# A convolution's first activation chunk moved from SyncE's DMA queue to ScalarE's

## The chip, the cores and the metric

The kernel runs on one core of a Trainium2 chip. TensorE multiplies matrices into PSUM; VectorE, ScalarE and GpSimd do elementwise work; SyncE only issues DMAs here. ScalarE and GpSimd can issue DMAs too, each into a queue of its own, and all queues use the same 16 DMA engines of the core. The metric is the device time of one execution in microseconds.

## The reference

A 3x3 convolution with zero padding, without bias, and then the maximum over 2x2 windows: the input `x` is 16 images of 64 channels of 64x64 in float32, the weights are 128x64x3x3, the output is 16x128x32x32.

```
conv[b, co] += weight[co, ci, kh, kw] * x_pad[b, ci, kh:kh+h, kw:kw+w]
output[b, c, i, j] = max(conv[b, c, 2*i:2*i+2, 2*j:2*j+2])
```

## The kernel before

Two images lie side by side on the 128 partitions (64 channels each), so TensorE works on two row halves at a time (the two "lanes" 0 and 1 in the order). Each of the eight pairs of images is cut into four chunks of 16 image rows, 32 chunks in all, numbered 0 to 31. The weights are not used as they come: sums and differences of their three kernel rows are formed first (the blocks G0, G1, G2, D0, D2, GM, GP), turned by TensorE (`T`), and copied back from PSUM as `wt` (`TV`). A chunk is done in one of two ways, given by the string `SEQ`. A W chunk uses sums and differences of image rows (E, S and V, tiles `we`, `ws`, `wv`), and takes four products, P0 to P3. A K chunk takes its rows as they are, cast to bfloat16 (`kx`), and takes five products (PAa, PAb, PBa, PBb, PR). The products of even output rows collect in one PSUM bank (A), those of odd rows in another (B). ScalarE copies bank A (`EV`, and `SE` as a seed into bank B), VectorE takes the maximum of the two (`MX`), ScalarE copies the odd columns (`OD`) and VectorE takes the maximum with the even ones (`CM`). `ST` stores.

The order of all work is written out by hand in the string `ORDER` (lines 16 to 80). Each token adds its instructions, so the order of the tokens is the order in which each engine and each queue meets its work; between engines semaphores do the rest. What the change and the prediction touch stands at its head:

- `LW` loads the weights (`wraw`, line 533) through SyncE.
- `c.X:e` forms block X on engine e (v VectorE, a ScalarE), line 196 or 191. GS is a sum (`gsum`) of which GM and GP are made.
- `LX.n` loads chunk n. For a W chunk it goes into the tile `wx`, line 262, on SyncE. Chunk 1 is the first W chunk: 17 rows, 544 KB. For K chunks 0 and 2 it goes into `kf`, line 268; chunk 0, the first five-product chunk, is loaded in two halves, `LX.0a` (288 KB) and `LX.0b` (256 KB). There the ending `:a` already chose ScalarE's queue, but no token used it.
- `E.1:v` is VectorE's first operation on chunk 1 (`we<-wx`), `V.1:v` the next one (`wv<-wx`). `P2.1.0` and `P2.1.1`, the first products, need E.1.
- `SE.1.0` seeds a bank. Where the bank has held nothing of the kind before, TensorE first writes zeros to it (`L430`) from the tile `zeros`.
- `XO.0b:a` and `XO.0a:v` cast chunk 0 to bfloat16 on ScalarE and VectorE.
- `CP.3` has ScalarE copy rows of W chunk 3 into a PSUM bank (line 287), for VectorE to read.

VectorE's order at the start is: the sum GS, D0, GM, D2, E.1, GP, V.1, the copy of GP (line 242), the cast XO.0a, two more copies. SyncE's is: weights, W chunk 1, chunk 0 in two halves, W chunk 3, chunk 2, and so on. The function `paced` makes loads wait for work far behind them; the loads named here have nothing to wait for.

Before the loop TensorE runs eight matmuls of ones (line 500). The table that ScalarE needs for its operations is loaded by an instruction that stands ahead of its first operation.

Of the kernel before, what the change touches and what calls it, by code (L numbers as in the profile page):

```python
# [13 lines left out]
SEQ = "KWKWWKWWWKWWWWKWWWKWWWWKWWWKWWWW"  # L14
ADDED = ()
ORDER = """
LW c.g1:a c.GS:v c.D0:v LX.1 c.GM:v c.D2:v LX.0a c.g0:a T.G0:0 T.GM:1 T.G1:2 E.1:v c.g2:a T.D2:3
TV.GM:a TV.G0:a T.G2:4 TV.D2:a LX.0b LX.3 P2.1.0:5 P2.1.1:6 TV.G2:a c.GP:v SE.1.0:7 V.1:v T.D0:1
LX.2 SE.1.1:0 T.GP:3 LX.4 TV.GP:v XO.0b:a XO.0a:v P0.1.1 P0.1.0 PAa.0.0a:4 PAa.0.1a:3 S.1:g P3.1.0
P3.1.1 TV.D0:v LX.8 XE.0a:a CP.3:1 PAa.0.1b PAb.0.0a TV.G1:v E.3:v S.3:v EV.1.1 EV.1.0 XE.0b:a  # L20
PAa.0.0b PAb.0.1a MX.1.1 PBa.0.1a:2 PBa.0.0a:6 PAb.0.0b PAb.0.1b V.3:g PBb.0.0a PBb.0.1a LX.6 XE.2:a
# [62 lines left out]
def kernel(  # L84
# [7 lines left out]
    nc = tc.nc  # L92
    FP32 = mybir.dt.float32
    BF16 = mybir.dt.bfloat16
# [13 lines left out]
    const = ctx.enter_context(tc.tile_pool(name="const", bufs=1))  # L108
# [16 lines left out]
    def behind(inst, other):  # L125
        if other is not None:
            tc.add_manual_dep(inst.ins, other.ins.name, SYNC, reason="order")
# [7 lines left out]
    def rows_of(p, lo, hi):  # L135
        return x[2 * p : 2 * p + 2].rearrange("b c h w -> (b c) h w")[:, lo:hi, :]

    def chunk(s):

        p, q = place[s]  # L140
        same = any(place[t] == (p, q - 1) and SEQ[t] == SEQ[s] for t in range(N))
        lo = 2 * R * q + 1 if same else max(0, 2 * R * q - 1)
        return p, lo, min(H, 2 * R * (q + 1) + 1)

    def half(s):
        return 2 * R * place[s][1] + R + 1
# [18 lines left out]
    wq = const.tile([CO, 7, 2, 2, CI], BF16)  # L165
    wt = const.tile([128, 7 * K, CO], BF16)
    gsum = const.tile([CO, 3, CI], FP32)
    zeros = const.tile([128, 512], BF16)
    nc.vector.memset(zeros, 0.0)
    ident = const.tile([128, 128], BF16)  # L170
    make_identity(nc, ident)
    wv = wraw.rearrange("a (c k) -> a k c", k=K * K)

    def ring(t, k):
# [69 lines left out]
            nc.vector.tensor_copy(out=dst, in_=src)  # L244


    kf = {}
    done = {}
    AHEAD = {"W": 12, "K": 13}

    def paced(s, inst):

        for l in (0, 1):
            behind(inst, done.get((s - AHEAD[SEQ[s]], l)))
        if SEQ[s] == "K" and s < AHEAD["K"] and s not in kf:
            behind(inst, done["head"])

    def load(s, part, e):
        p, lo, hi = chunk(s)
        if SEQ[s] == "W":  # L260
            t = wx[p % NWX]
            paced(s, nc.sync.dma_start(out=t[:, lo + 1 : hi + 1, :], in_=rows_of(p, lo, hi)))
            return
        if s not in kf:
            kf[s] = const.tile([128, hi - lo, W], FP32, name=f"kf_{s}")
        a, b = {"": (lo, hi), "a": (lo, half(s)), "b": (half(s), hi)}[part]
        q = nc.scalar if e == "a" else nc.sync
        paced(s, q.dma_start(out=kf[s][:, a - lo : b - lo, :], in_=rows_of(p, a, b)))

    def load_cast(s):  # L270
# [242 lines left out]
    for token in ORDER.split():  # L513
        what, _, at = token.partition(":")
        name, *args = what.split(".")
        if name in PRODUCTS:
            s, l = int(args[0]), int(args[1][0])
# [20 lines left out]
        elif name == "LX":  # L538
            load(int(args[0].rstrip("ab")), args[0].lstrip("0123456789"), at)
        elif name == "LK":  # L540
            load_cast(int(args[0]))
        elif name == "CP":
            lift(int(args[0]), int(at))
        elif name in ("XO", "XE"):
            to_bf16(int(args[0].rstrip("ab")), args[0].lstrip("0123456789"), int(name == "XO"), at)
        elif name in ("KS", "S", "E", "V"):
            f = rs_cast if name == "S" and int(args[0]) in ADDED else None
            (f or {"KS": ks, "S": rs, "E": re, "V": rv}[name])(int(args[0]), at)
        elif name in ("Ve", "Vo"):
            rv_half(int(args[0]), at, int(name == "Vo"))  # L550
        elif name == "SA":
            rs_add(int(args[0]))
        elif name == "ST":
            l, part = (int(args[1][0]), args[1][1:]) if len(args) > 1 else (None, "")
            store(int(args[0]), l, part, at)
        else:
            s = int(args[0])
            l, part = (int(args[1][0]), args[1][1:]) if len(args) > 1 else (None, "")
            if name in ("SE", "SEv"):
                bank["B", s, l] = int(at)  # L560
                seed(s, l, name[2:])
                continue
            if name in ("OD", "CM", "RM"):
                {"OD": odd, "CM": colmax, "RM": pairmax}[name](s, l, part)
            else:
                {"EV": evac, "MX": rowmax}[name](s, l)
# [36 lines left out]
```

## Time and profile before

| | us |
|---|---|
| Median of 3 runs | 104.27 (104.04 to 104.47) |
| The profiled execution | 103.89 |
| Its span, first to last instruction | 102.1 |
| TensorE busy | 95.6 |
| VectorE busy | 90.0 |
| ScalarE busy | 89.6 |
| GpSimd busy | 80.8 |

The profile's times count from the span's start. A timeline row gives the start, the length, the engine, the line, the operation with the tiles written and read (`out<-in`), and in square brackets the idle time of the engine before it with what ended it. `SPq` and `ACTq` are the queues of SyncE and ScalarE; the length of a DMA row is the time that its issue took. A row of a DMA list gives the size and the median time from the start of the issue to the landing. A row of a stretch gives its ends, its length, the busy time of PE, PEld (weight loads), DVE (VectorE), ACT (ScalarE) and POOL (GpSimd) with their instructions, TensorE's granted clock, the busy share of the DMA engines, and GB/s.

### The profile page before, as it was taken

The numbers are of one execution on the slowest core, as the hardware profiler recorded it, in microseconds if no ns is written. First come the engines' busy times: TensorE is split into PE (matmuls) and PEld (weight loads), VectorE is DVE, ScalarE is ACT, GpSimd is POOL, SyncE is SP. The second block draws the span as 40 slices with busy tenths as digits, with TensorE's granted clock in tenths as the row PEclk, the third lists the DMA queues.
The fourth block names the chain that finished last, engine by engine and source line by source line (L and its number), as shares of the span: only waits on it lengthen the run. The fifth ranks groups of instructions, "written<-read, shape, count | busy, mean of one in ns | idle before, by whom it ended". The sixth has DMA issues, their size and how long they took to land.

```text
span 102.1 us, 2481 instructions
## 1 busy us (share of the span) xinstructions
PE 95.6 (94%) x870; PEld 52.3 (51%) x870; DVE 90.0 (88%) x176; ACT 89.6 (88%) x200; POOL 80.8 (79%) x63
## 2 busy tenths in 40 slices
PE   6698999999999999999999999999999999999940
PEld 2155954555555567565555575555444446455310
DVE  1596999999989999999999999778989999998780
ACT  5597999888999999998899999999998988999930
POOL 5005998999599969999998999999971999999000
PEclk9999999999999999999999999999999999999999
DMA  2989999849940699999999971898769955302353
GB/s 42 343 235 414 418 419 335 181 113 356 263 122 0 165 219 324 250 322 328 255 404 350 377 287 28 251 251 219 282 213 311 340 179 180 128 32 74 132 182 103
DMA packets 13789, 24.07 MB, mean 236 GB/s; under 512 B 1104, under 2 KB 9680, under 8 KB 13776
## 3 DMA queue, kind: packets, MB, share of 16 engines
q1 hardware_dynamic: 12624, 22.16, 64.8%
q0 software_dynamic: 864, 1.56, 8.8%
q10 hardware_dynamic: 288, 0.20, 0.6%
q8 instruction: 7, 0.11, 0.4%
q14 instruction: 6, 0.05, 0.1%
HBM read 17.07 MB, written 8.39 MB: 249 GB/s over the span
## 4 chain that ended last, share of the span: by engine, by line
PE 84%; DVE 6%; DMA 3%; ACT 3%; issue 1%; ACTq 0%; DVEq 0%
PE acc L405 84%; DMA wraw<-in_weight_dram 3%; DVE wq L196 2%; ACT ev L420 1%; DVE wv L196 1%; ACT od L463 1%; DVE o L472 1%; DVE acc L440 1%; DVE we L196 1%; DVE gsum L196 0%; ACT acc L287 0%; ACT acc L436 0%; DVE wt L242 0%; DVE o L482 0%; ACTq L436 0%
## 5 line engine op out<-in xcount | busy, mean ns | idle before, releaser
L405 PEld LDWEIGHTS <-wt 64*128 64x128 bf16 x840 | 50.0, 94 | 40.6 <-issue 3.0
L405 PE MATMUL acc<-wv,wt 64*128 64x504 bf16 (+1 forms) x288 | 63.4, 377 | 0.5 <-DVE wt L242 0.5
L196 POOL TENSOR_TENSOR wv<-wx 128x1024 bf16<-128x1024 f32 x21 | 49.3, 2363 | 1.0 <-PE acc L405 0.4
L440 DVE TENSOR_TENSOR acc<-acc,ev 128x512 f32<-128x512 f32 x64 | 43.6, 692 | 2.7 <-ACT ev L420 1.4
L405 PE MATMUL acc<-kx,wt 64*128 64x504 bf16 (+6 forms) x216 | 38.6, 350 | 0.0
L405 PE MATMUL acc<-we,wt 64*128 64x512 bf16 (+1 forms) x144 | 36.9, 376 | 0.1
L405 PE MATMUL acc<-ws,wt 64*128 64x512 bf16 (+1 forms) x144 | 35.0, 377 | 0.2 <-DVE acc L440 0.2
L420 ACT ACTIVATE ev<-acc 128x512 f32<-128x512 f32 x48 | 28.8, 605 | 1.5 <-PE acc L405 1.2
L436 ACT COPY acc<-acc 128x512 f32<-128x512 f32 x48 | 28.2, 591 | 1.3 <-DVE o L472 0.4
L472 DVE TENSOR_TENSOR o<-acc,od 128x256 f32<-128x256 f32 x64 | 25.3, 414 | 2.1 <-ACT od L463 1.7
L463 ACT COPY od<-acc 128x256 f32<-128x256 f32 x64 | 23.0, 377 | 2.5 <-PE acc L405 1.2
L196 POOL TENSOR_TENSOR ws<-wx 128x512 bf16<-128x512 f32 x12 | 15.2, 1274 | 9.8 <-DVE kx L193 6.8
L196 POOL TENSOR_TENSOR we<-wx 128x512 bf16<-128x512 f32 x10 | 12.8, 1276 | 2.0 <-DVE ks L196 1.2
L405 PE MATMUL acc<-ks,wt 64*128 64x504 bf16 (+1 forms) x48 | 12.9, 376 | 0.0
L422 ACT COPY ev<-acc 128x512 f32<-128x512 f32 x16 | 9.3, 595 | 1.0 <-PE acc L405 0.8
L291 DVE TENSOR_TENSOR we<-acc,wx 128x512 bf16<-128x512 f32 x11 | 7.5, 683 | 1.2 <-ACT acc L287 1.1
L291 DVE TENSOR_TENSOR ws<-acc,wx 128x512 bf16<-128x512 f32 x11 | 7.5, 679 | 0.0
L287 ACT COPY acc<-wx 128x512 f32<-128x512 f32 x11 | 6.7, 606 | 0.6 <-DMA wx<-in_x_dram 0.6
L500 PE MATMUL acc<-const-bfloat16-1.0 128*128 128x512 bf16 x8 | 3.3, 585 | 0.8 <-PEq L584 0.8
L196 DVE TENSOR_TENSOR ks<-kx 128x512 bf16<-128x512 bf16 x8 | 4.0, 512 | 0.0
L196 DVE TENSOR_TENSOR wv<-wx 128x1024 bf16<-128x1024 f32 x3 | 3.7, 1217 | 0.0
L272 POOL DMA_DIRECT2D kx<-in_x_dram x6 | 3.5, 586 | 0.0
(28 smaller groups left out, 21.7 us busy)
## 6 DMA issues: line engine op xcount, KB each, us to landing
out_dram<-o SPq DMA_DIRECT2D x30, 256.0 KB, 3.5
wx<-in_x_dram SPq DMA_DIRECT2D x12, 512.0 KB, 7.1
wx<-in_x_dram SPq DMA_DIRECT2D x6, 544.0 KB, 5.1
wx<-in_x_dram SPq DMA_DIRECT2D x6, 480.0 KB, 7.7
kx<-in_x_dram POOLq DMA_DIRECT2D x3, 256.0 KB, 7.5
kf<-in_x_dram SPq DMA_DIRECT2D x1, 512.0 KB, 7.8
kx<-in_x_dram POOLq DMA_DIRECT2D x2, 240.0 KB, 7.8
wraw<-in_weight_dram SPq DMA_DIRECT2D x1, 288.0 KB, 3.0
```

Source lines behind the costliest of these rows:

```text
L196: inst = eng[e].tensor_tensor(out=out, in0=in0, in1=in1, op=op)
L272: paced(s, nc.gpsimd.dma_start(out=kx_of(p)[:, lo:hi, :], in_=rows_of(p, lo, hi)))
L287: nc.scalar.copy(out=acc[bank], in_=wrow(s, 0))
L291: nc.vector.tensor_tensor(out=t, in0=lifted[s], in1=wrow(s, 1), op=op)
L405: yield lambda kw=kw, o0=o0, o1=o1, c0=c0, c1=c1: nc.tensor.matmul(acc[t][:, i0:i1, o0:o1], wt[l * CI : l * CI + CI, K * BLOCKS[block] + T ...
L420: inst = nc.scalar.mul(t, acc[bank["A", s, l]], -1.0)
L422: inst = nc.scalar.copy(out=t, in_=acc[bank["A", s, l]])
L436: nc.scalar.copy(out=acc[b], in_=acc[bank["A", s, l]])
L440: nc.vector.tensor_tensor(out=t, in0=t, in1=ev[s, l], op=MAX)
L463: nc.scalar.copy(out=od[s, l][:, i0:i1], in_=acc[bank["B", s, l]][:, i0:i1, 1::2])
L472: done[s, l] = nc.vector.tensor_tensor(out=outs(s)[:, l, i0:i1], in0=acc[bank["B", s, l]][:, i0:i1, 0::2], in1=od[s, l][:, i0:i1], op=MAX,)
L500: nc.tensor.matmul(acc[n], ones[:, 0:128], ones, start=True, stop=True, skip_group_check=True)
```

## The change

The token `LX.1` becomes `LX.1:a`, and the two halves of chunk 0 move ahead of it. `load` learns to choose the queue for W chunks too. The tile `zeros` is no longer set by VectorE's memset but by a ScalarE multiplication by zero, which is now ScalarE's first operation, so the table load stands ahead of it and the DMA issue of chunk 1 behind both. SyncE's order becomes: weights, chunk 0 in two halves, W chunk 3, chunk 2, and so on as before. The order of the compute instructions on TensorE and GpSimd is unchanged; VectorE has one fewer and ScalarE one more.

```diff
 ORDER = """
-LW c.g1:a c.GS:v c.D0:v LX.1 c.GM:v c.D2:v LX.0a c.g0:a T.G0:0 T.GM:1 T.G1:2 E.1:v c.g2:a T.D2:3
-TV.GM:a TV.G0:a T.G2:4 TV.D2:a LX.0b LX.3 P2.1.0:5 P2.1.1:6 TV.G2:a c.GP:v SE.1.0:7 V.1:v T.D0:1
+LW LX.0a LX.0b LX.1:a c.g1:a c.GS:v c.D0:v c.GM:v c.D2:v c.g0:a T.G0:0 T.GM:1 T.G1:2 E.1:v c.g2:a
+T.D2:3 TV.GM:a TV.G0:a T.G2:4 TV.D2:a LX.3 P2.1.0:5 P2.1.1:6 TV.G2:a c.GP:v SE.1.0:7 V.1:v T.D0:1
...
-    zeros = const.tile([128, 512], BF16)
-    nc.vector.memset(zeros, 0.0)
     ident = const.tile([128, 128], BF16)
     make_identity(nc, ident)
+    zeros = const.tile([128, 512], BF16)
+    nc.scalar.mul(zeros, nc.const_aps.tensor(1.0, [128, 512], BF16), 0.0)
...
+    queue = {"s": nc.sync, "a": nc.scalar}
...
         if SEQ[s] == "W":
             t = wx[p % NWX]
-            paced(s, nc.sync.dma_start(out=t[:, lo + 1 : hi + 1, :], in_=rows_of(p, lo, hi)))
+            q = queue[e or "s"]
+            paced(s, q.dma_start(out=t[:, lo + 1 : hi + 1, :], in_=rows_of(p, lo, hi)))
             return
...
-        q = nc.scalar if e == "a" else nc.sync
+        q = queue[e or "s"]
         paced(s, q.dma_start(out=kf[s][:, a - lo : b - lo, :], in_=rows_of(p, a, b)))
```

## The prediction

> **What bounds the kernel now.** I read the page's head, then the chain of waits in order of time, then TensorE's own waits, then the first ten microseconds by engine, by DMA landing and by stretch.
>
> ```profile
> span 102.1 us, 2481 instructions
> PE 95.6 (94%) x870; PEld 52.3 (51%) x870; DVE 90.0 (88%) x176; ACT 89.6 (88%) x200; POOL 80.8 (79%) x63
> ```
>
> ```profile
> 0.74 3.02 DMA wraw<-in_weight_dram
> ...
> 3.79 0.51 DVE gsum L196
> 4.29 1.58 DVE wq L196 x3
> 5.87 0.60 DVE we L196
> 6.47 0.53 DVE wq L196
> 7.00 1.07 DVE wv L196
> ...
> 8.13 0.37 DVE wt L242
> 8.50 36.38 PE acc L405 x350
> ```
>
> ```profile
> 8.50:96.10 87.60, 87.55 (x826) 49.14 (x827) 81.97 (x160) 82.12 (x186) 79.49 (x49) 1.00 0.77 243
> ```
>
> The chain of waits says that the first 8.5 us are one unbroken string: the weights' load, then VectorE alone, step after step without a gap, until TensorE starts on its long run. The stretch 8.50 to 96.10 (its first number is the length, the second PE's busy time) shows TensorE busy 87.55 of 87.60 us at full clock (1.00). So the kernel is a start of 8.5 us, a TensorE run with nothing to take out, and a tail. Whatever moves 8.50 moves the end by as much; what speeds up VectorE, ScalarE or a DMA behind 8.50 is worth nothing unless it is in one of TensorE's few small gaps.
>
> TensorE's own waits in the list for 8.4 to 96 us are one row, and it is the start itself:
>
> ```profile
> PE acc L405 <- DVE wt L242: 0.5, 1, 0.5
> ```
>
> The change works on what VectorE reads in those 8.5 us. Its timeline and the landings (the last number: microseconds from issue to landing), with the issues of SyncE (SPq) and ScalarE's work:
>
> ```profile
> 3.79 0.51 DVE L196 TENSOR_TENSOR gsum<-wraw 128x192 f32<-128x192 f32 x1 [2.65 <-DMA wraw<-in_weight_dram]
> ...
> 5.26 0.61 DVE L196 TENSOR_TENSOR wq<-wraw 128x256 bf16<-128x256 f32 x1
> 5.79 0.68 DVE L196 TENSOR_TENSOR we<-wx 128x512 bf16<-128x512 f32 x1
> ```
>
> ```profile
> 0.74 0.37 SPq L533 DMA_DIRECT2D wraw<-in_weight_dram  x1
> 1.17 0.42 SPq L262 DMA_DIRECT2D wx<-in_x_dram  x1
> 1.64 0.90 SPq L268 DMA_DIRECT2D kf<-in_x_dram  x2
> ```
>
> ```profile
> wraw<-in_weight_dram SPq DMA_DIRECT2D x1, 288.0 KB, 3.0
> ```
>
> ```profile
> wx<-in_x_dram SPq DMA_DIRECT2D x1, 544.0 KB, 4.4
> kf<-in_x_dram SPq DMA_DIRECT2D x1, 288.0 KB, 5.8
> ```
>
> ```profile
> kf<-in_x_dram SPq DMA_DIRECT2D x1, 256.0 KB, 6.2
> ```
>
> The weights land at 0.74 + 3.0 = 3.76 (the chain's end of that step), VectorE starts 0.03 later. The first W chunk (the tile `wx`, 544 KB) lands at 1.17 + 4.4 = 5.57, and its first reader, the operation E.1 (`we<-wx`), starts at 5.79, straight after the operation before it: the chunk is 5.79 - 0.03 - 5.57 = 0.19 us early. That is all the slack there is. The two halves of the first five-product chunk (`kf`) land at 1.64 + 5.8 = 7.44 and about 1.64 + 0.45 + 6.2 = 8.3.
>
> **The change, part by part.**
>
> *The zeros.* VectorE loses a memset; ScalarE gains a multiply of 128x512, behind the table load.
>
> ```profile
> 0.87 0.27 DVE L169 MEMSET zeros<- 128x256 uint32 x1 [0.87 <-PEq L584]
> ```
>
> ```profile
> 0.74 1.28 ACT L191 ACT_TABLE_LOAD   x1 [0.74 <-PEq L584]
> 3.79 1.75 ACT L191 CAST wq<-wraw 128x256 bf16<-128x256 f32 x3 [1.76 <-DMA wraw<-in_weight_dram]
> ...
> 9.68 0.59 ACT L287 COPY acc<-wx 128x512 f32<-128x512 f32 x1 [0.56 <-DMA wx<-in_x_dram]
> ```
>
> ```profile
> 7.46 0.38 PE L430 MATMUL acc<-zeros 128*128 128x512 bf16 x1
> ```
>
> The memset's 0.27 us lie in VectorE's wait for the weights (2.65 us after it), so its removal gains 0. ScalarE is free from 2.02 to 3.79; a multiply of about 0.6 us (its 128x512 copy at 9.68 took 0.59) and one DMA issue (0.42 by SyncE's row) end by about 3.1. If that cover were gone the casts of the weights would start late; 0.7 us of it are left. The only reader, TensorE's zero matmul, comes at 7.46. Cost 0. Moving the identity's making on GpSimd one line up changes no order there. Cost 0.
>
> *SyncE's queue.* With the W chunk gone the `kf` halves are issued at 1.17 and 1.64 instead of 1.64 and 2.11, and every later load 0.47 earlier. Who gains? The halves' readers stand behind E.1, V.1 and the step at 8.13 on VectorE and behind the seeds on ScalarE; TensorE's row above shows it waiting for none of them. The next W chunk is waited for, by the copy at 9.68 (0.56 us); an earlier landing there gives ScalarE up to 0.56 us back, but TensorE runs without a wait across it. Gain 0, with at most a few tenths in later gaps.
>
> *The W chunk on ScalarE's queue.* This is the one part on the path. It is issued behind the table load, so at 2.02 or a little later instead of 1.17. I take 2.05: the last DMAs of the kernel show that ScalarE's queue issues while the instruction just ahead of it still runs.
>
> ```profile
> 98.94 0.27 ACT L463 COPY od<-acc 128x128 f32<-128x128 f32 x1 [0.82 <-DVE o L482]
> 98.94 0.96 ACTq L495 DMA_DIRECT2D out_dram<-o  x2
> ```
>
> If it must wait for the multiply's end it is 2.6, 0.55 later. The first data follow an issue by about 1 us (weights issued at 0.74; the stretch 1.50 to 1.75 below is the first with any), so the chunk's data begin at about 3.05. In the rows below the last number is GB/s, the one before it the DMA engines' busy share.
>
> ```profile
> 1.50:1.75 0.25, 0.25 (x2) 0.15 (x1) 0.00 (x0) 0.25 (x1) 0.17 (x2) 1.00 0.03 9
> 1.75:2.00 0.25, 0.25 (x2) 0.00 (x0) 0.00 (x0) 0.25 (x1) 0.21 (x1) 1.00 1.96 240
> 2.00:2.25 0.25, 0.25 (x2) 0.15 (x1) 0.00 (x0) 0.02 (x1) 0.00 (x0) 1.00 0.65 55
> 2.25:2.50 0.25, 0.25 (x2) 0.06 (x1) 0.00 (x0) 0.00 (x0) 0.00 (x0) 1.00 0.19 65
> ...
> 4.50:5.00 0.50, 0.00 (x0) 0.00 (x0) 0.50 (x2) 0.50 (x2) 0.00 (x0) 1.00 1.21 239
> 5.00:5.50 0.50, 0.44 (x5) 0.27 (x6) 0.50 (x2) 0.50 (x1) 0.00 (x0) 1.00 0.84 184
> 5.50:6.00 0.50, 0.48 (x8) 0.31 (x8) 0.50 (x2) 0.26 (x2) 0.00 (x0) 1.00 0.67 123
> 6.00:6.50 0.50, 0.44 (x6) 0.35 (x7) 0.50 (x2) 0.50 (x2) 0.00 (x0) 1.00 0.97 177
> ...
> 9.00:9.50 0.50, 0.50 (x12) 0.40 (x10) 0.22 (x1) 0.13 (x1) 0.50 (x1) 1.00 1.04 426
> ```
>
> In the queue of before the chunk's data went alone, straight behind the weights. Now `kf` stands there, and the chunk comes from a second queue onto the same 16 DMA engines. How two queues share is seen where GpSimd's queue (q0) and SyncE's (q1) both have work, in the microsecond 17 to 18 (packets, MB, share of the engines):
>
> ```profile
> q0 software_dynamic: 59, 0.12, 63.5%
> q1 hardware_dynamic: 46, 0.17, 44.0%
> ```
>
> They take turns, about packet by packet (59 to 46), and the shares add to the whole: nothing is moved on the side. A packet is one partition's line of a load (46 packets of 0.17 MB are 3.7 KB each), 128 in the chunk and 128 in each `kf` half, so by the time the chunk is through, the first half has gone as well: 288 + 544 + 288 = 1120 KB, against 832 KB before. That gives the two ends of its landing.
> Upper end: before, exactly those 1120 KB had landed with the first `kf` half at 7.44, slow stretch of 4.5 to 6.5 included (123 to 239 GB/s). E.1 would wait 7.44 - 5.76 = 1.68 us.
> Lower end: no slow stretch. Up to 2.5 some 0.25 x (9 + 240 + 55 + 65) = 92 kB had moved; the other 1055 kB at the full rate of 426 GB/s take 2.5 us: 5.0, and with an allowance of 0.3 to 0.5 from last byte to landing, 5.3 to 5.5. E.1 would wait for nothing.
> The slow stretch of before is the very time in which `kf` was moved (between the landings at 5.57 and 8.3), and `kf` is moved again, only sooner; but part of the slowness may belong to the time and not to the data. I take the middle, 6.45, and a wait of 6.45 - 5.76 = 0.7 us.
>
> [...]
>
> *What follows a late E.1.* Behind it on VectorE stand the GP block's sum, V.1 and the copy at 8.13, all on the chain, so 8.50 becomes 9.20. TensorE's first products need E.1's result directly. ScalarE's seeds wait for those. VectorE and ScalarE take their later idle time (the 0.56 above) as cover, TensorE has none. The removed slack is 0.19, the new wait 0.7, all on the path.
>
> Sum: 0 (zeros) + 0 (SyncE) + 0.7 (W chunk) = +0.7 us. The profiled execution took 103.89 (span 102.1 and 1.79 around it), so 104.6 by it; it lay 0.38 under the median of the runs, and on the median of 104.27 the sum is 104.95.
>
> **The rivals.**
>
> *In time after all.* The chunk lands by 5.76: the lower end above. For it: the slow stretch may not come back, and 5.3 to 5.5 leaves 0.2 to 0.4. Against it: any slow half microsecond uses that up. Time: 104.27.
>
> *The table load holds nothing back (the change does not do what it says).* If ScalarE's queue runs past the table load, the issue comes at about 0.8 and the chunk takes turns with the weights themselves. The weights are then through when most of the 832 KB are: 544 KB more before them, 1.3 us at 426 GB/s, at most 5.57 - 3.76 = 1.8. All of the chain moves by that: 105.6 to 106.1, say 105.85. For it: the 98.94 rows, where the DMA did not wait for the copy ahead. Against it: two instructions stand ahead here, and the table load starts at 0.74 together with SyncE's DMA issue, as something that the queue itself does. [...]
>
> *The table load costs more than its row.* ScalarE might be held beyond 2.02, with the issue at 3 or later, and its casts delayed too: landing past 7.2 and 105.8 or more. The row of 3.79 only shows it free by then. [...]
>
> *Faster.* The weights stall: 55 and 65 GB/s from 2.00 to 2.50, against 426 when the queue flows. If that is because a 544 KB load is being put in the queue right behind them (issued 1.17 to 1.59), a 288 KB one there could give back up to that half microsecond: weights at 3.26, chain 0.5 earlier, 103.75. It decides only if the W chunk is in by 5.26, so it needs the share of the engines to be better than turn by turn, or no slow stretch. Against it: those are the first data of all, and a cold start would be as slow with any successor.
>
> **How the numbers follow.** Forecast (late W chunk, 0.3 to 1.7 us): 0.50, own range 104.5 to 105.9. In time: 0.22. Past the table load: 0.12. Longer table load: 0.04. Faster: 0.12. Half a per cent, 0.52 us, is about what a measurement tells here. Slower by more: three quarters of the forecast and both table-load cases, 0.38 + 0.16 = 0.54. Within: 0.22 and the rest of the forecast, 0.34. Faster: 0.12. Predicted 104.95. The range leaves out most of "faster" and the far ends: 103.9 to 106.0.
>
> **What would show it.** Right: an ACTq issue of `wx` at 2.0 to 2.1; its landing over 4 us later, at 6 or more; in VectorE's timeline, E.1 with a wait for the DMA of `wx` in front; TensorE's run beginning about 9.2 instead of 8.50 and as long as before; the chain's string broken by that DMA. Wrong: E.1 straight behind the operation before it (in time); the ACTq issue at 0.8 and the weights landing near 5 (past the table load); weights before 3.5 (faster). The sum would also fail if TensorE's run itself became longer or shorter than 87.6 us.

## The result, and the profile after

| | before | changed |
|---|---|---|
| Median of 20 runs each | 104.16 us | 105.64 us |
| Lowest and highest | 103.52 to 105.29 | 104.47 to 107.34 |
| The profiled execution, and its span | 103.89, 102.1 | 105.81, 103.9 |

The changed kernel is slower: the ratio is 1.0121, with a 95% interval from 1.0093 to 1.015, so about 1.3 us. The ratio is that of the means without each kernel's slowest executions (those over 1.5% above its fastest), and so not quite the quotient of the two medians. The twenty runs of the changed kernel fall into groups: three lie at 104.47 to 104.83, the rest at 105.39 and above, with nothing in between. The profiled execution is one of the second group.

The queues of the changed kernel come first. ScalarE's timeline:

```profile
0.73 1.28 ACT L171 ACT_TABLE_LOAD   x1 [0.73 <-PEq L586]
0.80 0.38 ACTq L264 DMA_DIRECT2D wx<-in_x_dram  x1
2.03 0.63 ACT L171 ACTIVATE zeros<-const-bfloat16-1.0 128x512 bf16<-128x512 bf16 x1
4.98 1.75 ACT L191 CAST wq<-wraw 128x256 bf16<-128x256 f32 x3 [2.33 <-DMA wraw<-in_weight_dram]
```

The load of the W chunk stands behind the table load and the multiplication in ScalarE's order, and is issued at 0.80, while the table load runs and 1.2 us before the multiplication begins. So it is issued beside SyncE's load of the weights (0.74), not behind it. The two loads' landings (last number, from the start of the issue):

```profile
wx<-in_x_dram ACTq DMA_DIRECT2D x1, 544.0 KB, 4.9
wraw<-in_weight_dram SPq DMA_DIRECT2D x1, 288.0 KB, 4.2
```

The weights take 4.2 us where they took 3.0. The W chunk is in at 0.80 + 4.9 = 5.7, hardly later than before (5.57). What the DMA engines did between 3 and 4 us (packets, MB, share of the engines; q10 is ScalarE's queue, q1 SyncE's):

```profile
q10 hardware_dynamic: 58, 0.25, 62.2%
q1 hardware_dynamic: 54, 0.12, 35.3%
```

They took turns, 58 packets to 54, and since a packet of the chunk is nearly twice as long (0.25 MB in 58 packets are 4.3 KB each, 0.12 MB in 54 are 2.2), the weights had a third of the engines, 35.3% against 62.2%. Now VectorE and TensorE:

```profile
4.99 0.50 DVE L196 TENSOR_TENSOR gsum<-wraw 128x192 f32<-128x192 f32 x1 [4.99 <-DMA wraw<-in_weight_dram]
...
6.97 0.70 DVE L196 TENSOR_TENSOR we<-wx 128x512 bf16<-128x512 f32 x1
...
10.16 0.36 DVE L242 TENSOR_SCALAR wt<-acc 128x384 bf16<-128x384 bf16 x1 [0.83 <-PE acc L229]
```

```profile
0.78 3.57 PE L502 MATMUL acc<-const-bfloat16-1.0 128*128 128x512 bf16 x8 [0.78 <-PEq L586]
6.23 1.83 PE L229 MATMUL acc<-ident,wq 128*128 128x128 bf16 x15 [1.88 <-ACT wq L191]
7.99 1.39 PE L407 MATMUL acc<-we,wt 64*128 64x512 bf16 x6
...
10.53 0.82 PE L407 MATMUL acc<-wv,wt 64*128 64x512 bf16 x6 [0.49 <-DVE wt L242]
```

The same groups of TensorE in the kernel before:

```profile
5.04 1.40 PE L229 MATMUL acc<-ident,wq 128*128 128x128 bf16 x15 [0.97 <-ACT wq L191]
6.53 0.82 PE L405 MATMUL acc<-we,wt 64*128 64x512 bf16 x6
```

VectorE starts 4.99 - 3.79 = 1.20 us later, and E.1 stands straight behind the operation before it: it waits for no W chunk. A second loss follows. TensorE's first 15 transposes take 1.83 us instead of 1.40 and its first six products 1.39 instead of 0.82, as at a lower clock. The trace's record of TensorE's clock bears this out: its first stretch of full clock begins at 9.19 us in the changed kernel and at 3.65 in the kernel before. At 10.16 VectorE has waited 0.83 us for TensorE. TensorE's long run begins at 10.53 instead of 8.50: 2.03 us later, of which 1.20 are the weights and 0.83 this. In the chain of waits, what follows the weights is now ScalarE's casts and TensorE's slow transposes and products, where before it was VectorE's work. From 10.80 to 19.20 it runs through GpSimd, whose first operation there starts 2.02 us later than before (10.80 against 8.78). It ends with the same steps as before, at 98.67 for the last three products against 96.89, so 1.78 of the 2.03 arrive:

```profile
0.74 4.22 DMA wraw<-in_weight_dram
...
4.98 1.20 ACT wq L191 x2
...
6.23 1.83 PE acc L229 x15
8.06 1.32 PE acc L407 x4
...
10.80 1.27 POOL ws L196
...
19.25 27.43 PE acc L407 x250
...
98.67 0.83 PE acc L407 x3
```

```profile
96.89 0.83 PE acc L405 x3
```

(The first of these two fences is the changed kernel, the second the kernel before.)

### The profile page after: what moved, and what is told of

Read it like the earlier page. It is cut to its first block, busy times and chain, and to the rows that moved or that the text cites. A ratio compares the mean times of both kernels' runs of the same rounds, so it can differ in the third digit from the quotient of the medians.

```text
span 103.9 us, 2481 instructions
## 1 busy us (share of the span) xinstructions
PE 96.5 (93%) x870; PEld 52.7 (51%) x870; DVE 90.0 (87%) x175; ACT 90.4 (87%) x201; POOL 80.8 (78%) x63
## 4 chain that ended last, share of the span: by engine, by line
PE 78%; POOL 7%; DMA 4%; ACT 4%; DVE 2%; issue 2%; DVEq 0%; ACTq 0%
PE acc L407 75%; DMA wraw<-in_weight_dram 4%; POOL wv L196 4%; POOL ws L196 2%; PE acc L229 2%; ACT wq L191 1%; ACT ev L422 1%; POOL kx L274 1%; ACT od L465 1%; DVE o L474 1%; DVE acc L442 1%; ACT acc L289 0%; ACT acc L438 0%; DVE o L484 0%; DVE kx L193 0%
## 5 line engine op out<-in xcount | busy, mean ns | idle before, releaser
L407 PE MATMUL acc<-we,wt 64*128 64x512 bf16 (+1 forms) x144 | 37.4, 386 | 0.0
L196 DVE TENSOR_TENSOR gsum<-wraw 128x192 f32<-128x192 f32 x1 | 0.5, 501 | 5.0 <-DMA wraw<-in_weight_dram 5.0
L229 PE MATMUL acc<-ident,wq 128*128 128x128 bf16 x21 | 2.5, 285 | 1.9 <-ACT wq L191 1.9
```

The costliest lines, as they stand in the source:

```text
L196: inst = eng[e].tensor_tensor(out=out, in0=in0, in1=in1, op=op)
L229: nc.tensor.transpose(tp[:, (j - lo) * 128 : (j - lo + 1) * 128], wq[:, BLOCKS[m]].rearrange("a i j c -> a (i j c)")[:, (j - lo) * CI : (j ...
L407: yield lambda kw=kw, o0=o0, o1=o1, c0=c0, c1=c1: nc.tensor.matmul(acc[t][:, i0:i1, o0:o1], wt[l * CI : l * CI + CI, K * BLOCKS[block] + T ...
```

## The experiments

**The price of sharing, by a smaller share.** Only 9 of the chunk's 17 rows go by ScalarE's queue, the other 8 by SyncE's right behind the weights.

```diff
-LW LX.0a LX.0b LX.1:a c.g1:a ...
+LW LX.1b LX.0a LX.0b LX.1a:a c.g1:a ...
...
+            a, b = {"": (lo, hi), "a": (lo, half(s)), "b": (half(s), hi)}[part]
-            paced(s, q.dma_start(out=t[:, lo + 1 : hi + 1, :], in_=rows_of(p, lo, hi)))
+            paced(s, q.dma_start(out=t[:, a + 1 : b + 1, :], in_=rows_of(p, a, b)))
```

> Only the first 9 of the W chunk's 17 rows (288 KB) go by ScalarE's queue at 0.80, the other 8 by SyncE's right behind the weights. Theory (turn by turn, 8 packets of each load on a DMA engine): between the weights' packets stand the same number of packets, each of 93 ns instead of 168, so the weights are late by about 8 x 93 ns = 0.7 us instead of 1.2 to 1.3: landing at 4.4 to 4.5, and the time about 0.7 us above before, more if TensorE starts cold. Rival (the delay does not hang on the bytes, but on a second queue being there): landing at 4.9 to 5.0 as in the changed kernel.

The weights' landing in its chain of waits:

```profile
0.74 3.49 DMA wraw<-in_weight_dram
```

They land at 4.23: 0.47 us late instead of 1.20, with half the bytes beside them. The expectation was 0.7; the direction and the order of size are those of packets taking turns, and a delay that comes with the mere presence of a second queue (4.9 to 5.0) is excluded. The ratio of times is 1.0071 (1.0022 to 1.0121), but it is not the price of sharing alone: in this profile, too, the transposes take 1.82 us and the first products 1.46, and VectorE waits 0.99 us for TensorE.

**The load truly held.** The W chunk's issue waits for the end of the multiplication.

```diff
-    nc.scalar.mul(zeros, nc.const_aps.tensor(1.0, [128, 512], BF16), 0.0)
+    zeroed = nc.scalar.mul(zeros, nc.const_aps.tensor(1.0, [128, 512], BF16), 0.0)
...
-            paced(s, q.dma_start(out=t[:, lo + 1 : hi + 1, :], in_=rows_of(p, lo, hi)))
+            inst = q.dma_start(out=t[:, lo + 1 : hi + 1, :], in_=rows_of(p, lo, hi))
+            if e == "a":
+                behind(inst, zeroed)
+            paced(s, inst)
```

> The W chunk's issue on ScalarE's queue waits for the end of the multiplication by zero, so it comes at about 2.7 instead of 0.80; all else is the changed kernel. Theory (the chunk's packets take turns with the weights' packets, and that is what made the weights late): the weights land at 3.7 to 3.9 again instead of 4.96. The chunk, now behind the weights but turn by turn with the first five-product chunk, lands at 6.3 to 7.5, and E.1 waits 0.5 to 1.7 us for it, as the prediction had it; the time is 0.5 to 1.7 us above before. Rival (a load that is issued by ScalarE, or the five-product chunk right behind the weights on SyncE's queue, makes the weights late in itself): the weights stay at 4.7 or later.

VectorE's timeline and ScalarE's queue:

```profile
3.69 0.50 DVE L196 TENSOR_TENSOR gsum<-wraw 128x192 f32<-128x192 f32 x1 [3.69 <-DMA wraw<-in_weight_dram]
...
10.38 0.69 DVE L196 TENSOR_TENSOR we<-wx 128x512 bf16<-128x512 f32 x1 [4.61 <-DMA wx<-in_x_dram]
```

```profile
2.69 0.38 ACTq L264 DMA_DIRECT2D wx<-in_x_dram  x1
```

```profile
wx<-in_x_dram ACTq DMA_DIRECT2D x1, 544.0 KB, 7.7
```

The first half of the expectation holds: with the chunk out of the way the weights land at about 3.67 again (3.69 less the 0.02 or 0.03 from landing to start), so it was the chunk's company that made them late, and nothing in the new order of SyncE's queue. The second half is wrong by far: the chunk takes 7.7 us from its issue and lands at 10.35, E.1 waits 4.61 us, and the time is 110.1 us, 5.8 above before where 0.5 to 1.7 was expected, ratio 1.0556 (1.0462 to 1.065).

**Why the held chunk was so late.** As above, but SyncE's queue issues nothing behind the two halves of chunk 0 until the W chunk has landed.

```diff
             if e == "a":
                 behind(inst, zeroed)
+                done["first"] = inst
+            if s == 3:
+                behind(inst, done["first"])
```

> As e1_held (the W chunk's issue on ScalarE's queue waits for the multiplication), but SyncE's queue issues nothing behind the two halves of the first five-product chunk until the W chunk has landed. It tells why the chunk of e1_held took 7.7 us. Theory (its packets stood behind and between the 512 KB loads that SyncE's queue had already issued): without them the first data come within 1.3 us of the issue and the chunk lands at 5.3 to 6.5, 2.6 to 3.8 us after its issue. Rival (a load on ScalarE's queue is slow when it is issued while SyncE issues its own, or the 2 us to its first data belong to that queue): first data again 2 us after the issue, landing at 7 or later.

The landing, and the stretches from 4 us on (last number GB/s, before it the DMA engines' busy share):

```profile
wx<-in_x_dram ACTq DMA_DIRECT2D x1, 544.0 KB, 4.9
```

```profile
5.00:5.50 0.50, 0.50 (x5) 0.38 (x6) 0.50 (x2) 0.48 (x1) 0.00 (x0) 1.00 1.04 313
...
6.00:6.50 0.50, 0.50 (x8) 0.50 (x6) 0.00 (x0) 0.50 (x2) 0.00 (x0) 1.00 0.47 192
6.50:7.00 0.50, 0.28 (x3) 0.13 (x2) 0.00 (x0) 0.50 (x3) 0.00 (x0) 1.00 0.27 113
```

It lands at 7.55, 2.8 us sooner than with SyncE's loads beside it, so those loads were 2.8 of the 7.7 us. But neither side of the expectation holds whole: the 4.9 us are more than the theory's 2.6 to 3.8, and the rival has the late landing right (7 or later) but not its reason, first data 2 us after the issue. The second half of chunk 0 is in by about 5.2; from 6 us on, nothing but the chunk is to be moved and yet the engines are busy 47% and then 27% of the time. Whether part of them are through while others are still at the chunk, the rows do not tell. Its first packet begins at 4.16, 1.5 us after the issue (2.3 us in the run above); the first packet of the weights comes 1.0 us after theirs. What delayed the chunk's first packets stays open. The one run took 106.73 us.

**The zeros alone**, in the kernel before:

```diff
-    zeros = const.tile([128, 512], BF16)
-    nc.vector.memset(zeros, 0.0)
     ident = const.tile([128, 128], BF16)
     make_identity(nc, ident)
+    zeros = const.tile([128, 512], BF16)
+    nc.scalar.mul(zeros, nc.const_aps.tensor(1.0, [128, 512], BF16), 0.0)
```

> The kernel before with the tile of zeros set by ScalarE's multiplication instead of VectorE's memset, nothing else. Theory: no change, ratio 0.995 to 1.005, the weights land at 3.7 to 3.8 and VectorE's first sum starts right behind. Rival (the multiplication holds ScalarE's casts or the table load shifts something): slower by 0.3 us or more, with a gap before the casts that the weights do not end.

Ratio 1.0012 (0.9968 to 1.0056), VectorE's first sum at 3.80: no change that can be told.

**TensorE's clock, in the changed kernel.** More matmuls of ones ahead of the loop fill TensorE's pause, and so also lengthen the time that it is busy.

```diff
-    for n in range(8):
+    for n in range(12):
         nc.tensor.matmul(
-            acc[n], ones[:, 0:128], ones, start=True, stop=True, skip_group_check=True
+            acc[n % 8], ones[:, 0:128], ones, start=True, stop=True, skip_group_check=True
```

> The changed kernel with 12 instead of 8 matmuls of ones ahead of the loop, so that TensorE is busy until about 5.2 (full clock) to 5.9 (half clock) instead of 4.35. Theory (in the profiled execution of the changed kernel the pause from 4.35 to 6.23 kept TensorE at half clock until 9.19, which cost 0.8 us on top of the weights' 1.2): full clock is granted before 6.3, the 15 transposes take 1.4 us instead of 1.83 and the first six products 0.82 instead of 1.39, VectorE does not wait 0.8 us for the transposes, and the time falls by up to 0.8 us below the changed kernel, to about 1.2 us above before. The weights still land at 4.9 to 5.0. Rival (the clock has nothing to do with the pause): the slow transposes and products stay and the time is that of the changed kernel.

```profile
0.78 4.96 PE L502 MATMUL acc<-const-bfloat16-1.0 128*128 128x512 bf16 x12 [0.78 <-PEq L586]
6.06 1.41 PE L229 MATMUL acc<-ident,wq 128*128 128x128 bf16 x15 [0.32 <-ACT wq L191]
7.55 0.82 PE L407 MATMUL acc<-we,wt 64*128 64x512 bf16 x6
```

The transposes and the first products have their old lengths, the record of the clock has full clock from 5.29 on, and VectorE no longer waits for TensorE ahead of the copy of GP. The weights still land late (0.74 + 4.04 = 4.78 in its chain). The median is 104.57, the ratio 1.0039 (1.0003 to 1.0075): about 0.4 us above before, not the 1.2 expected. The profiled execution, the slowest of the ten, is 0.8 us longer than that of before (spans of 102.9 and 102.1). The lowest runs are as far apart, 104.36 and 103.56. The kernel before also has runs up to 105.1, which raise its mean and which the twelve matmuls do not have; that may be why the ratio is so small. The ten runs lie within 104.36 to 104.77: the upper group of the changed kernel is gone, its lower group is left.

**TensorE's clock, in the kernel before.** The eight matmuls of ones use half of the array each, by turns, and end 1.4 us sooner. So TensorE is busy for a shorter time and then pauses for longer.

```diff
-            acc[n], ones[:, 0:128], ones, start=True, ...
+            acc[n], ones[n % 2 * CI : n % 2 * CI + CI, 0:128], ones[n % 2 * CI : n % 2 * CI + CI], start=True, ...
```

> The kernel before, but the eight matmuls of ones use 64 rows each, by turns the upper and the lower half of the array, so that they take some 1.8 us instead of 3.3 and TensorE then pauses for 2.5 us or more ahead of the transposes; loads and all else as before. Theory (a pause ahead of the first transposes costs about 1 us by the half clock): the weights land at 3.7 to 3.9, the transposes take about 1.8 us instead of 1.4, the first products 1.4 instead of 0.82, VectorE waits 0.6 to 0.9 us for TensorE ahead of the copy of GP, and nearly all runs are 0.8 to 1.1 us above before. Rival (the eight matmuls do not set the clock): ratio 0.997 to 1.003.

```profile
0.78 1.89 PE L500 MATMUL acc<-const-bfloat16-1.0 64*128 64x512 bf16 x8 [0.78 <-PEq L584]
4.95 1.82 PE L229 MATMUL acc<-ident,wq 128*128 128x128 bf16 x15 [2.28 <-ACT wq L191]
6.71 1.46 PE L405 MATMUL acc<-we,wt 64*128 64x512 bf16 x6
```

With no load changed, and the weights in at 3.68, the transposes take 1.82 and the products 1.46, and VectorE waits 1.3 us for TensorE, longer than the 0.6 to 0.9 expected. Full clock is on record from 8.94 only. Ratio 1.0071 (1.0036 to 1.0106), about 0.74 us, a little under the 0.8 to 1.1 expected. So the second loss is TensorE's own and needs no late load. The shorter busy time and the longer pause change together here, so the run does not say which of the two counts, and the length of the pause alone does not decide: two runs of other experiments have the same 3.57 us of ones, with a pause of 0.64 (the chunk held alone) and of 0.59 (the last run below), and transposes of 1.79 and 1.40.

```profile
4.99 1.79 PE L229 MATMUL acc<-ident,wq 128*128 128x128 bf16 x15 [0.64 <-ACT wq L191]
```

```profile
4.95 1.40 PE L229 MATMUL acc<-ident,wq 128*128 128x128 bf16 x15 [0.59 <-ACT wq L191]
```

That lengths like these are the clock can be seen in the run with the chunk held alone. Its first group of six products takes 0.82 us where the stretch reads clock 1.00 (third number from the end), its second 1.46 where it reads 0.50:

```profile
8.32 0.82 PE L413 MATMUL acc<-we,wt 64*128 64x512 bf16 x6 [1.54 <-DVE we L196]
...
10.29 1.46 PE L413 MATMUL acc<-wv,wt 64*128 64x512 bf16 x6 [0.49 <-DVE wt L242]
```

```profile
8.30:9.10 0.80, 0.78 (x7) 0.25 (x7) 0.80 (x2) 0.00 (x0) 0.00 (x0) 1.00 0.52 138
10.10:13.40 3.30, 3.11 (x18) 1.51 (x19) 1.89 (x6) 2.42 (x7) 2.84 (x2) 0.50 0.92 264
```

By what rule the clock is granted, these runs do not show. That the same kernel gets full clock sooner in one run and later in another is the author's estimate; it would fit the two groups of runs (104.47 to 104.83, 105.39 and above), their joining when the pause is filled (104.36 to 104.77), and the unequal transposes (1.79 and 1.40) behind equal matmuls of ones (3.57). In the run with the chunk held alone the clock's record has 3.41 us of full clock and then 3.41 of half. No run of the lower group was profiled.

**The same filling, in the kernel before** (10 matmuls of ones instead of 8, by the same edit): the version that might beat both.

> The kernel before with 10 matmuls of ones instead of 8, which keeps TensorE busy until about 4.5 (full clock) to 5.1 (half clock) instead of 4.07; nothing else. Theory (some runs of the kernel before, those near 105.0 us, are runs in which full clock came too late, as in most runs of the changed kernel): those runs disappear, the rest stay at 103.6 to 104.4, the median is equal or up to 0.3 us lower, ratio 0.996 to 1.001. Rival (the runs near 105 have another cause): they stay, ratio 0.999 to 1.003.

Median 104.28 against 104.29, ratio 0.9986 (0.9951 to 1.0021): not to be told from the kernel before. Two of its twelve runs lie above 105 us (105.55 and 106.76), so it does not rid the kernel of all such runs; whether it makes them fewer can't be said at this size.

**The reorder alone**, all on SyncE's queue:

```diff
-LW c.g1:a c.GS:v c.D0:v LX.1 c.GM:v c.D2:v LX.0a c.g0:a ...
+LW LX.0a LX.0b LX.1 c.g1:a c.GS:v c.D0:v c.GM:v c.D2:v c.g0:a ...
```

> The reorder alone: all loads on SyncE's queue, the two halves of the first five-product chunk ahead of the W chunk, zeros as before. Theory: the weights land at 3.6 to 3.8 as before, the W chunk behind 1376 KB at 8.0 to 8.8, E.1 waits 2.2 to 3.0 us for it, and the time rises by that and, where the pause of TensorE costs it its clock, by 1 us more: 2.2 to 4 us above before. Rival (what is read from the late chunk is hidden by other work): less than 1 us.

```profile
9.21 0.69 DVE L196 TENSOR_TENSOR we<-wx 128x512 bf16<-128x512 f32 x1 [3.61 <-DMA wx<-in_x_dram]
...
9.81 0.61 DVE L196 TENSOR_TENSOR wq<-gsum,wraw 128x256 bf16<-128x256 f32 x1
```

The weights are in at 3.50; the W chunk comes at 9.18, later than the 8.0 to 8.8 expected, and E.1 waits 3.61 us. Median 109.11, ratio 1.0457 (1.0393 to 1.0521), 4.8 us over before where 2.2 to 4 was expected: the wait and more, since TensorE loses its clock here, too (its first products take 1.47 us, at a granted clock of 0.50). Here nothing hides the late W chunk.

**Whose the slow stretch is.** The kernel before, with SyncE's issue of chunk 0's first half held until the W chunk has landed.

```diff
+            inst = nc.sync.dma_start(out=t[:, lo + 1 : hi + 1, :], in_=rows_of(p, lo, hi))
+            done.setdefault("first", inst)
...
+        if s == 0 and part == "a":
+            behind(inst, done["first"])
```

> The kernel before, but SyncE issues the first half of the first five-product chunk only when the W chunk has landed, at about 5.6 instead of 1.64, and all later loads behind it. It asks whose the slow stretch of 4.5 to 6.5 us (123 to 239 GB/s) is, on which the prediction's upper bound rested. If it belongs to the first load from another part of the input (the five-product chunk comes from the first pair of images, the W chunk from the third), it comes again with these loads: below 250 GB/s on the average of the first 1.5 us from their first data at about 6.6, and the 1056 KB of the two halves and the next W chunk take 4 us or more. If it belongs to the time and not to the load, the rate reaches 350 GB/s or more within half a microsecond of those first data. The W chunk lands at 5.3 to 5.6 either way. The time is not of interest here; the late chunk makes it slower by 1 us or more.

```profile
6.50:7.00 0.50, 0.50 (x6) 0.16 (x5) 0.50 (x2) 0.50 (x3) 0.00 (x0) 1.00 1.08 217
7.00:7.50 0.50, 0.50 (x8) 0.28 (x5) 0.50 (x1) 0.50 (x2) 0.00 (x0) 1.00 0.85 210
7.50:8.00 0.50, 0.42 (x5) 0.15 (x2) 0.50 (x1) 0.50 (x2) 0.00 (x0) 1.00 1.00 269
8.00:8.50 0.50, 0.09 (x2) 0.18 (x4) 0.50 (x3) 0.36 (x1) 0.00 (x0) 1.00 0.91 270
```

The slowness moves with the loads: 217, 210 and 269 GB/s in the first three of these half microseconds, and the next W chunk is in 4.9 us after its issue. So in this one run it does not belong to the time 4.5 to 6.5. That it belongs to a new part of the input is not shown: in this run the queue was empty ahead of the loads, and the weights, the first load of all, begin as slowly (240, 55 and 65 GB/s in the three quarters of a microsecond from 1.75 on, in the kernel before).

## Why the prediction came out as it did

The measured 105.64 lies within the range of 103.9 to 106.0 and on the predicted side, but not by the forecast's mechanism, so the fit of the forecast's number is luck. What happened is the rival "the table load holds nothing back", which had a chance of 0.12 and a price of 105.85.

- *The weights lead the chain, and nothing but the start matters.* Right: the chain begins with the weights' load in both kernels, and the start's delay of 2.03 us comes through as 1.78. It said "all on the path"; about a quarter of a microsecond is regained after 10.53. Part of that seems to come from the next W chunk. ScalarE's copy of it waits 0.56 us for its landing in the kernel before and not at all in the changed one; the 30 products of chunk 0 that TensorE does meanwhile take 1.87 us before and 1.74 changed.
- *The zeros cost nothing.* Right: 1.0012 by themselves.
- *SyncE's later loads gain nothing.* Right in effect. The first half of chunk 0 even lands at 1.18 + 6.3 = 7.5, as before (7.44), though it was issued 0.46 us sooner:

```profile
kf<-in_x_dram SPq DMA_DIRECT2D x1, 288.0 KB, 6.3
```

- *"It is issued behind the table load, so at 2.02 or a little later instead of 1.17. I take 2.05."* This is the step that failed. The issue came at 0.80. The prediction had the right row in hand (at 98.94 a DMA was issued while the copy ahead of it ran) and set it aside because the table load starts as early as SyncE's issue, "as something that the queue itself does". In the order that the kernel's text gives, the DMA stands behind the table load and the multiplication; it was issued before the first had ended and before the second had begun, so the order alone held it behind neither. (The trace shows times, not ScalarE's list itself; that the list keeps the order of the text is taken from the kernel.) So the table load held nothing back: 0.80 against its end at 2.01.
- *The rival's price.* It said that the weights would be 1.3 to 1.8 us late; they were 1.20. It said nothing of TensorE's clock, which is the missing term: 0.83 in the profiled execution. That the rival's price came near, too, is a matter of one term too large and one left out. By ratios, the late weights alone (twelve matmuls of ones) cost 0.39% and the half clock alone (short matmuls of ones in the kernel before) 0.71%; together 1.10%, against 1.21% measured, well within the intervals, which are wide. In the spans of the profiled executions it is 0.8 and 1.0 us, against 1.8.
- *"The table load costs more than its row."* It did not: the multiplication begins at 2.03, 0.02 us behind the table load's end. No run shows the issue at 3 or later on which the price of this rival stood: it came at 0.80, and at 2.69 where it was made to wait for the multiplication.
- *Two queues take turns packet by packet.* Right: 58 to 54, and half the chunk beside the weights makes them 0.47 us late.
- *Had the issue been late,* the forecast's +0.7 and its upper end of 1.68 would probably have been far too low: the held run, with its issue at 2.69 instead of the forecast's 2.05, came to +5.8 us, with 4.61 of waiting. The step at fault is "by the time the chunk is through, the first half has gone as well: 288 + 544 + 288 = 1120 KB". In the held run both halves had landed long before the chunk (at 4.4 and 6.1), and it shared the engines with the 512 KB loads behind them; without these it still took 4.9 us:

```profile
kf<-in_x_dram SPq DMA_DIRECT2D x1, 288.0 KB, 3.2
kf<-in_x_dram SPq DMA_DIRECT2D x1, 256.0 KB, 4.5
```

- *The slow stretch.* The guess that part of it belongs to the time fell: it moves with the loads.
- *"Faster", by a shorter stall of the weights.* Little of it: with the 288 KB half right behind them and no chunk beside them the weights land at 3.50 (the reorder alone), 3.67 and 3.71 (the two held runs), against 3.68 to 3.77 in the runs with the old order; at most a quarter, not the half microsecond.

## What to carry to other kernels

Here a DMA that stood behind a computation in an engine's program order was not held by it (issued at 0.80, with the table load ending at 2.01 and the multiplication beginning at 2.03). If a load must come later, give it something to wait for, and then look at what has been queued ahead of it (held to 2.69, the chunk took 7.7 us, and 4.9 without the loads of SyncE's queue behind chunk 0). The second queue gave no bandwidth here (370 GB/s from 3 to 4 us, against 387 in the kernel before): its packets took turns, 58 to 54, with those of the load that everything waited for, which landed 1.20 us later, so keep the load at the head of the chain alone on the engines where you can. When a start is delayed, look at TensorE's clock as well: here 0.83 us of waiting for slow transposes and products came on top of the 1.20.

## What the runs showed of the hardware

- A load from ScalarE's queue, issued while SyncE's queue was at work, had its first packet 1.5 to 2.3 us after the start of its issue (1.6 in the changed kernel, 2.3 in the held run, 1.5 with SyncE's later loads held back), against 1.0 for the weights on the idle engines. And with the engines to itself at the end it left them idle most of the time (47%, then 27% busy). The cause was not found.
- Eight matmuls of ones, 3.3 to 3.6 us, sometimes brought TensorE to full clock ahead of the transposes and sometimes did not. The transposes took 1.40 us behind a pause of 0.97 us in the kernel before and of 0.59 in the last run, but 1.83 behind 1.88 in the changed kernel and 1.79 behind 0.64 with the chunk held alone. From run to run of the changed kernel the time fell into two groups (104.47 to 104.83, or 105.39 and up). Twelve matmuls, which left a pause of 0.32 us, took away the upper group in ten runs.
- The clock column of the stretches reads 1.00 ahead of the trace's first record of the clock, also where TensorE was slow (until 9.19 in the changed kernel); there only the lengths of its instructions show the clock. Later stretches show it: 0.50 where six products took 1.46 us, 1.00 where they took 0.82.
